# A hybrid decoder layer on one core: five blocks of one 426-column tile in place of three blocks of two 355-column tiles, with the small weight parts kept in HBM

## The chip, the core and the metric

The kernel runs on one core of a Trainium2 chip. The metric is the device time of one execution in microseconds (us); the runs of the kernel before give 3005.64 to 3007.39, median 3006.2. The profile shows one execution by engine: PE (matrix products), PEld (the loads of its weights), DVE (vector), ACT (scalar), POOL, and SP, which here issues all DMA transfers in order.

## What is computed

One layer of a decoder for 2,064 prompt rows (16 meta tokens and 2,048) and 8 × 8 sample rows, 2,128 rows in all, 1,024 channels, float32. Cut to what matters:

```python
h = rmsnorm(x, norm1_g)
z = h @ w_in                                   # 1024 -> 5 x 1024
a = za * sigmoid(zg)                           # GLU
a = layernorm(causal_dwconv(a, width 31) + conv_b)
a = silu(a) @ w_conv_out
p = multiscale_pool(zp)                        # trailing means over 2, 4, 8, 16 rows, less the row
p = einsum(p by 4 groups, w_pool) * pool_scale
m = sigmoid(gate_a) * a + sigmoid(gate_b) * p
x = x + m @ w_out
h2 = rmsnorm(x, norm2_g)
up = causal_dwconv(h2 @ w_up, width 3)         # 1024 -> 2 x 2816
x = x + (gelu(g) * v) @ w_down
y = rmsnorm(x, final_g)
```

The last rows of each causal operation are outputs too.

## The kernel before

Channels lie on the 128 partitions, in chunks; rows of x are the columns of every tile. The columns are cut into three blocks of 708, 708 and 712 (`WIDTHS`), each of two column tiles of 354 or 356, which lie in the two banks of one PSUM tile (4 of these). The sample rows are in block 2 (`SBLK`).

Every float32 operand of a product is held as two float32r parts: a rounded part and the rest, `hi` and `lo` for activations, `wh` and `wl` for weights. `gemm` makes three products per 128 channels of depth, wl·hi, wh·lo and wh·hi. For a weight of 1,024 channels by 128 outputs (512 KB) and one block these are 24 products for each of the two column tiles. Weights are loaded anew in each block: `w_loads` issues the load into `raw`, `w_split` lets ACT copy it to `wh` and DVE subtract it to `wl`, up to four weights ahead (`LEAD`).

The products are in units, one per output chunk: G (gate and value of the convolution branch), PG (pooling input, `w_pool`, merge gates), C (`w_conv_out`), WO (`w_out`), and FF, which is made of up-projections and of groups of the down-projection, DN. `join` lets the first few units of a stage run in turn, chunk by chunk, as their operands come about. Before the first block's norms and around the second norm of blocks 0 and 2 the two column tiles go one after the other (`SPLIT`): the products of one run while the other's norm is made. Block 1's G shares weights with block 0's in `G_first`.

A norm squares the chunks on ACT, adds them on DVE (`sumsq`), and in `rstd_ps` takes sums over partitions by small float32 matmuls with `ones`, ten small DVE operations on a tile `rs`, and small matmuls with the unit matrix in `cst`; `rstd_of` copies the result by ACT. `norm1_rstd` (task r1) and `h_make` (tasks h1 and h1b) make the first norm of a block, `norm2` the second, `conv_norm` and `silu` the convolution branch's, `final` the last one. The normalized x of a block is dropped after G and made again for PG (h1b), from loads of x.

The order of all work is written by the program itself: units in a list, and beside them tasks that are stepped by a forecast of each engine's time (`Pace`, `drip`, `force`). A unit that needs a task forces it to its end before its first product, so the task's small matmuls come ahead of these products in the PE's order. On SP a raw load waits until the split of the weight that had its place is done.

Of the kernel before, what the change touches and what calls it, by code (L numbers as in the profile page):

```python
# [32 lines left out]
NBLK = 3  # L33
SBLK = 2
TOT = NP_ALL + NSAMP
_W = TOT // NBLK // 4 * 4
WIDTHS = [_W + 4 * (i >= NBLK - (TOT - NBLK * _W) // 4) for i in range(NBLK)]
assert sum(WIDTHS) == TOT and all(w % 4 == 0 for w in WIDTHS)
# [10 lines left out]
S_SLOTS = 52  # L49
S_COLS = max(HC + WMAX, WMAX + 2)  # L50
W_BUFS = 4
RAW_BUFS = 2
F_GROUPS = (6, 5, 5, 6)
LEAD = 4
# [3 lines left out]
RESERVE = 3  # L58
# [3 lines left out]
LAST_GROUPS = (8, 7, 7)  # L62
OWN = 4
POOL_ORDER = (1, 0, 3, 2)
BOTH, FIRST, SECOND = (0, 1), (0,), (1,)
SPLIT = (FIRST, SECOND)
# [50 lines left out]

class Task:
# [5 lines left out]
def trunk(ctx: ExitStack, tc: tile.TileContext, A, O):  # L124
# [5 lines left out]
    ppool = ctx.enter_context(tc.tile_pool(name="ppool", bufs=4, space=bass.MemoryType.PSUM))  # L130
# [16 lines left out]
    def room(k):  # L147
        """Waits until k more tiles fit, beside a few for the work that can't wait."""

        def ok():  # L150
            held[:] = [t for t in held if sys.getrefcount(t) > 3]
            return len(held) + k <= S_SLOTS - RESERVE

        if not ok():
            yield "room", ok

    def PSUM():
        return pace.alloc("ps", 4, ppool.tile([P, 2, 512], F32, tag="ps", name=nm("ps")))
# [58 lines left out]
    def hw(b):  # L217
        return WIDTHS[b] // 2

    def cols(b, ts_):  # L220
        return ts_[0] * hw(b), (ts_[-1] + 1) * hw(b)

    def sb(ap, b, ts_):
        """The columns of a tile that belong to the column tiles ts_, in the shape of ps_of."""
        c0, c1 = cols(b, ts_)
        return ap[:, c0:c1].rearrange("p (a c) -> p a c", a=len(ts_))

    def ps_of(ps, b, ts_, off=0):
        return ps[:, : len(ts_), off : off + hw(b)]

    R = {}

# [1 line left out]
    wq = []  # L234
    wsplits = {}
    wstate = {"load": 0, "split": 0, "done": 0}

    def w_loads():
        while wstate["load"] < min(len(wq), wstate["done"] + RAW_BUFS):
            src, n = wq[wstate["load"]][:2]  # L240
            raw = pace.alloc("raw", RAW_BUFS, wpool.tile([P, n], F32, tag="raw", name=nm("raw"), bufs=RAW_BUFS))
            load(raw, src)
            wq[wstate["load"]].append(raw)
            wstate["load"] += 1

    def w_split(i):
        while len(wq[i]) < 3:
            yield "cond", lambda: len(wq[i]) > 2
        n, raw = wq[i][1], wq[i][2]
        wh = pace.alloc("wh", W_BUFS, wpool.tile([P, n], F32R, tag="wh", name=nm("wh")))  # L250
        wl = pace.alloc("wl", W_BUFS, wpool.tile([P, n], F32R, tag="wl", name=nm("wl")))
        wq[i].append((wh, wl))
        yield "at", max(pace.ready(wh), pace.ready(raw))
        act(wh, raw, AF.Copy)
        yield at(wh)
        tt(wl, raw, wh.bitcast(F32), ALU.subtract)
        wstate["done"] += 1
        w_loads()

    def w_start(first):  # L260
        w_loads()
# [5 lines left out]
    def w_ahead(i, first):  # L267
        """Weights up to number i are split when this returns; more are under way, first is the oldest still in use."""
# [10 lines left out]
    def gemm(ps, w, pairs, rng, woff=0):  # L279
# [12 lines left out]
    def rng(b, ts_, halo=0):  # L292
        h = hw(b)
        return [(t * h, (t + 1) * h + halo) for t in ts_]

# [4 lines left out]
    def rsums(acc, n):  # L300
        """Mean over all channels of acc, whose columns [0, n) hold sums over the channel chunks, on every partition."""
        ps = PSUM()
        k = 1 if n <= 512 else 2
        for t in range(k):
            mm(ps[:, t, : n // k], ones, acc[:, t * (n // k) : (t + 1) * (n // k)], True, True, 4.0)
        return ps[:, :k, : n // k]

    def rstd_ps(src, n):
        """1 / sqrt(mean of squares + eps) of each column, on every partition.

        The columns' sums go to a column on their own partition each, there a first guess from the exponent, a step of
        third order and a Newton step follow, and a product with the unit matrix takes the result to all partitions."""
        acc = yield from sumsq(src, n)
        yield at(acc)
        halves = 1 if n <= 512 else 2
        h = n // halves
        cuts = [(t, c) for t in range(halves) for c in [*range(0, h - P + 1, P)] + [h - P] * (h % P > 0)]
        k = len(cuts)
        ps = PSUM()
        for j, (t, c) in enumerate(cuts):  # L320
            mm(ps[:, 0, j : j + 1], acc[:, t * h + c : t * h + c + P], ones[:, :1], True, True, 64.0)
# [4 lines left out]
        ts(v, ps[:, 0, :k], EPS, None, ALU.add)  # L326
# [9 lines left out]
        for j, (t, c) in enumerate(cuts):  # L336
            mm(ps[:, t, c : c + P], w[:, 1, j : j + 1].to_broadcast([P, P]), cst[:, O_ID : O_ID + P], True, True, 4.0)
        yield at(ps)
        return ps[:, :halves, :h]

    def rstd_of(src, n):
# [3 lines left out]
        act(wide(out, ps), ps, AF.Copy)  # L345
# [3 lines left out]
    def wide(x, ps):  # L349
        return x.rearrange("p (a c) -> p a c", a=ps.shape[1])  # L350

    def sumsq(src, n):
        """Squares of the chunks, summed; each chunk is added after the start of the next."""
# [24 lines left out]
    def staggered(first):  # L378
        """The rest after rounding, of chunk after chunk, each one after the start of the next."""
# [15 lines left out]
    def norm1_first(ts_):  # L395
        """First norm of block 0, one column tile at a time."""
        c0, c1 = cols(0, ts_)
        xs = [x_load(0, c, c0, c1) for c in range(KC)]
# [6 lines left out]
        r = yield from rstd_of(src, c1 - c0)  # L405
        if ts_[0] == 0:
            R["h", 0] = [(S(WIDTHS[0], F32R), S(WIDTHS[0], F32R)) for _ in range(KC)]

        def first(c):
            stt(xs[c], xs[c], col(O_N1 + c), r, ALU.mult, ALU.mult)  # L410
            act(R["h", 0][c][0][:, c0:c1], xs[c], AF.Copy)
            return xs[c], *(x[:, c0:c1] for x in R["h", 0][c])
# [43 lines left out]
    def past(b, key, c, rows, src, bufs):  # L456
        """The loader of a chunk's rows before the sample rows, in the block that holds these."""
# [10 lines left out]
    def gate_post(b, c, ts_, ps):  # L468
        if ts_[0] == 0:
            R["t", b, c] = S(WIDTHS[b])  # L470
        act(sb(R["t", b, c], b, ts_), ps_of(ps, b, ts_), AF.Tanh, scale=0.5)
        yield

    def value_post(b, c, ts_, ps):
        n, h, t = NPB[b], hw(b), R["t", b, c]
        if ts_[0] == 0:
            a = S(HC + n)
            pcopy(a[:, :HC], ahist[:, c, :])
            R["a", b, c] = [a, None, 0]
# [800 lines left out]
```

## Time and profile before

| | us |
|---|---|
| median of 3 runs (lowest, highest) | 3006.2 (3005.64, 3007.39) |
| span of the profiled execution | 3004.0 |
| PE busy | 2963.5 |
| DVE busy | 2162.5 |
| ACT busy | 970.3 |
| POOL busy | 87.9 |
| DMA share, moved | 25.4%, 251.6 MB |

The profiled execution's span is 2.2 us less than the median of the runs, which also hold what lies around the span. The PE's records overlap by the depth of its pipeline (a record lasts 326 ns, and one begins every 163), so the time of a product is read from starts or from the count in a stretch. Where PE waited, a row names the engine, tile and line that released it.

```profile
PE   7999999999999999999999999999999999999998
DVE  7999998789899856633698899986763366535356
ACT  4212234343222333522332322333352244313132
DMA  4211221422221223123332122222322242222223
```

Each digit is the busy share, in tenths, of a fortieth of the span.

### The profile page before, as it was taken

What the parts mean: (1) busy time and instruction counts of PE and PEld (TensorE: products, weight loads), DVE (VectorE), ACT (ScalarE), POOL (GpSimd) and SP (SyncE); (2) the same over time, 40 slices, a digit from 0 to 9 for tenths busy, and PEclk for the clock granted to TensorE, in tenths of its full rate; (3) what the DMA queues carried; (4) which work ended last, traced back from release to release, by engine and by line L of the source; (5) the groups of instructions that cost most, each with busy time, mean ns of one, the idle gap of its engine ahead of it and who ended that gap; (6) DMA issues with size and microseconds to landing.
All of it is one profiled execution on the core that took longest, in us unless ns stands there. A gap on an engine that the chain in (4) does not pass through costs nothing.

```text
span 3004.0 us, 43514 instructions
## 1 busy us (share of the span) xinstructions
PE 2963.5 (99%) x18156; PEld 2956.5 (98%) x18156; DVE 2162.5 (72%) x2958; ACT 970.3 (32%) x1311; POOL 87.9 (3%) x185
## 2 busy tenths in 40 slices
PE   7999999999999999999999999999999999999998
PEld 7999999999999999999999999999999999999998
DVE  7999998789899856633698899986763366535356
ACT  4212234343222333522332322333352244313132
POOL 0111000010000000000010000000000000000000
PEclk9999999999999999999999999999999999999999
DMA  4211221422221223123332122222322242222223
GB/s 166 75 36 60 71 70 47 156 80 60 74 71 55 79 86 119 64 78 117 122 99 68 61 80 65 66 74 75 122 86 77 96 137 74 79 68 77 71 77 114
DMA packets 95235, 251.64 MB, mean 84 GB/s; under 512 B 22080, under 2 KB 30400, under 8 KB 95040
## 3 DMA queue, kind: packets, MB, share of 16 engines
q1 hardware_dynamic: 95040, 248.88, 25.4%
q8 instruction: 142, 2.33, 0.3%
q14 instruction: 53, 0.43, 0.0%
HBM read 236.09 MB, written 12.75 MB: 83 GB/s over the span
## 4 chain that ended last, share of the span: by engine, by line
PE 97%; DVE 2%; ACT 1%; issue 0%; DMA 0%; SPq 0%; DVEq 0%; ACTq 0%
PE ps L200 97%; DVE s L171 1%; ACT s L183 1%; DVE s L167 1%; DMA s<-in_x 0%; DVE rs L171 0%; DVE wl L167 0%; ACT wh L183 0%; DVE rs L167 0%; SPq L192 0%; DVE rs L179 0%; DVE uw L167 0%; DVE rs L177 0%; DVEq L1258 0%; ACTq L183 0%
## 5 line engine op out<-in xcount | busy, mean ns | idle before, releaser
L200 PE MATMUL ps<-s,wh 128*128 128x354 f32 (+2 forms) x11904 | 2907.9, 326 | 8.0 <-DVE s L167 7.9
L200 PEld LDWEIGHTS ps<-s,wh 128*128 128x128 f32 x11904 | 2097.9, 189 | 10.7 <-DVE s L167 10.4
L200 PE MATMUL ps<-s,wl 128*128 128x356 f32 (+2 forms) x5952 | 1944.6, 327 | 6.8 <-ACT s L183 3.7
L200 PEld LDWEIGHTS ps<-s,wl 128*128 128x128 f32 x5952 | 1122.8, 189 | 8.9 <-ACT s L183 7.3
L171 DVE SCALAR_TENSOR_TENSOR s<-s,half,s 128x708 f32<-128x708 f32 (+1 forms) x720 | 626.7, 928 | 0.0
L167 DVE TENSOR_TENSOR wl<-raw,wh 128x1024 fp32r<-128x1024 f32 (+4 forms) x416 | 476.6, 1147 | 193.2 <-ACT wh L183 190.3
L183 ACT ACTIVATE wh<-raw 128x1024 fp32r<-128x1024 f32 (+4 forms) x416 | 412.3, 994 | 550.6 <-PE ps L200 410.5
L183 ACT ACTIVATE s<-s 128x708 fp32r<-128x708 f32 (+7 forms) x424 | 296.7, 710 | 548.0 <-DVE s L171 397.1
L167 DVE TENSOR_TENSOR s<-s,s 128x708 f32<-128x708 f32 (+7 forms) x453 | 358.5, 801 | 93.6 <-ACT s L183 89.4
L171 DVE SCALAR_TENSOR_TENSOR s<-ps,cst,s 128x708 f32<-128x708 f32 (+3 forms) x276 | 254.6, 924 | 189.4 <-ACT sf L183 109.7
L183 ACT ACTIVATE s<-ps,cst 128x708 f32<-128x708 f32 (+3 forms) x138 | 113.5, 825 | 457.6 <-PE ps L200 457.6
L167 DVE TENSOR_TENSOR s<-s,ps 128x708 f32<-128x708 f32 (+3 forms) x160 | 123.1, 779 | 144.9 <-PE ps L200 144.1
L183 ACT ACTIVATE s<-ps 128x708 f32<-128x708 f32 (+3 forms) x121 | 82.5, 690 | 396.4 <-PE ps L200 396.3
L171 DVE SCALAR_TENSOR_TENSOR s<-s,s 128x708 f32<-128x708 f32 (+2 forms) x96 | 85.3, 891 | 44.0 <-ACT s L183 42.4
L171 DVE SCALAR_TENSOR_TENSOR s<-s,ps 128x708 f32<-128x708 f32 (+5 forms) x65 | 44.0, 698 | 91.2 <-PE ps L200 90.5
L171 DVE SCALAR_TENSOR_TENSOR s<-s,cst,s 128x708 f32<-128x708 f32 (+3 forms) x112 | 83.5, 767 | 27.9 <-ACT s L183 14.8
L167 DVE TENSOR_TENSOR s<-s 128x722 f32<-128x722 f32 (+7 forms) x60 | 53.2, 886 | 17.0 <-ACT s L183 15.6
L171 DVE SCALAR_TENSOR_TENSOR sc<-sa,cst,sc 128x64 f32<-128x64 f32 x232 | 47.1, 278 | 0.3
L183 ACT ACTIVATE s<-s,half 128x708 f32<-128x708 f32 (+1 forms) x48 | 46.5, 975 | 0.8
L188 POOL COPY s<-phist 128x15 f32<-128x15 f32 x24 | 12.8, 534 | 1014.8 <-ACT s L183 1007.3
L188 POOL CAST s<-hhist 128x2 fp32r<-128x2 f32 x48 | 19.2, 416 | 642.9 <-PE ps L200 555.3
L200 PEld LDWEIGHTS ps<-ones,s 128*128 128x128 f32 x144 | 18.6, 197 | 11.8 <-issue 11.7
(43 smaller groups left out, 273.4 us busy)
## 6 DMA issues: line engine op xcount, KB each, us to landing
raw<-in_w_up SPq DMA_DIRECT2D x132, 512.0 KB, 3.3
raw<-in_w_in SPq DMA_DIRECT2D x112, 512.0 KB, 3.3
raw<-in_w_out SPq DMA_DIRECT2D x40, 512.0 KB, 3.3
s<-in_x SPq DMA_DIRECT2D x40, 354.0 KB, 6.1
raw<-in_w_co SPq DMA_DIRECT2D x24, 512.0 KB, 3.3
raw<-in_w_dn SPq DMA_DIRECT2D x32, 384.0 KB, 3.1
s<-in_x SPq DMA_DIRECT2D x32, 356.0 KB, 5.9
raw<-in_w_dn SPq DMA_DIRECT2D x24, 448.0 KB, 3.4
```

Source lines behind the costliest of these rows:

```text
L167: nc.vector.tensor_tensor(out=out, in0=a, in1=b, op=op)
L171: nc.vector.scalar_tensor_tensor(out=out, in0=a, scalar=s, in1=b, op0=op0, op1=op1)
L183: nc.scalar.activation(out, a, func, **kw)
L188: nc.gpsimd.tensor_copy(out, a)
L200: nc.tensor.matmul(out, lhsT=lhsT, rhs=rhs, start=start, stop=stop)
```

## The change

There are five blocks of 424, 426, 426, 426 and 426 columns, one column tile each, so that a unit has 24 products of one width. PSUM has eight tiles of one bank; there are 5 places for `wh` and `wl` (before 4), 3 for `raw` (2), 76 for activations (52). The halves (`SPLIT`, `G_first`) are gone: every norm covers its whole block.

A weight's `wl` is computed when the weight is used first (136 subtracts in place of 416) and stored to a tile `keep_` in HBM (136 stores); the other 544 uses load it back straight into `wl`. `wh` is copied by ACT from `raw` at each of the 680 uses (416 before).

The order of the stages is new: G(0), PG(0), G(1), PG(1), C(0), WO(0), FF(0), C(1), WO(1), G(2), FF(1), PG(2), C(2), WO(2), G(3), FF(2), PG(3), C(3), WO(3), G(4), FF(3) without its last DN group, PG(4), C(4), WO(4), that group, FF(4). silu of blocks 0 and 1 may begin eight units ahead of C (two before, in block 0). The task h1b, which begins at `mark["up_end", b]`, begins in block 4 right at PG(4), since no DN group stands there any more.

```diff
-NBLK = 3
-SBLK = 2
+NBLK = 5
+SBLK = NBLK - 1
+WIDTHS = [424, 426, 426, 426, 426]
-S_SLOTS = 52
+S_SLOTS = 76
-W_BUFS = 4
-RAW_BUFS = 2
+W_BUFS = 5
+RAW_BUFS = 3
+PS_BUFS = 8
-LEAD = 4
+LEAD = W_BUFS
-RESERVE = 3
+RESERVE = 4
...
+            q.lo = pace.alloc("wl", W_BUFS, wpool.tile([P, n], F32R, tag="wl", name=nm("wl")))
+            q.known = q.key in kept
+            if q.known:
+                load(q.lo.bitcast(F32), kept[q.key])
...
+        act(q.hi, q.raw, AF.Copy)
+        if not q.known:
+            yield at(q.hi)
+            tt(q.lo, q.raw, q.hi.bitcast(F32), ALU.subtract)
+            if q.again:
+                stores.append(q)
...
+        if len(stores) > 1 or (stores and q.known):
+            p = stores.pop(0)
+            kept[p.key] = dpool.tile([P, p.n], F32, tag=f"keep_{len(kept)}", name=f"keep_{len(kept)}")
+            store(kept[p.key], p.lo.bitcast(F32))
...
-            for i, (c0, c1) in enumerate(rng):
-                o = ps[:, i, : c1 - c0]
-                mm(o, wl[:, w0 : w0 + P], xh[:, c0:c1], k == 0, False)
-                mm(o, wh[:, w0 : w0 + P], xl[:, c0:c1], False, False)
-                mm(o, wh[:, w0 : w0 + P], xh[:, c0:c1], False, k == last)
+            o = ps[:, : c1 - c0]
+            mm(o, wl[:, w0 : w0 + P], xh[:, c0:c1], k == 0, False)
+            mm(o, wh[:, w0 : w0 + P], xl[:, c0:c1], False, False)
+            mm(o, wh[:, w0 : w0 + P], xh[:, c0:c1], False, k == last)
...
+    G(0, H1(0), False)
+    PG(0, H1(0), False)
+    mark["G", 1] = len(units)
+    G(1, H1(1), False)
+    PG(1, H1(1), False)
+    for b in range(NBLK):
+        if b > 1:
+            PG(b, H1B(b), True)
+        C(b)
+        WO(b)
+        if b == NBLK - 1:
+            DN(b - 1, *late)
+        elif b:
+            mark["G", b + 1] = len(units)
+            G(b + 1, H1(b + 1), True)
+        else:
+            mark["G", 2] = len(units)
+        late = FF(b, b == NBLK - 2)
...
-        add_task(("s", b), silu(b), mark["mid", b] if b else mark["C", 0] - 2, [("cv", b)])
+        add_task(("s", b), silu(b), mark["mid", b] if b > 1 else mark["C", b] - 8, [("cv", b)])
```

What this makes of the order is seen on PE where WO(1) passes into G(2). Before, `ps_12457` is the first norm of block 2, made inside WO(1), and `ps_12861` the second norm of block 1, made inside G(2); `ps_12464` and `ps_12542` are products of WO(1), `ps_12777` and `ps_12793` of G(2):

```order
L200 MATMUL ps_12394<-s_12168,wh_12158 128x354
L200 MATMUL ps_12457<-ones,s_12307 128x1 x6
L200 MATMUL ps_12464<-s_11393,wl_12239 128x354
...
L200 MATMUL ps_12464<-s_12168,wh_12158 128x354
L200 MATMUL ps_12457<-cst,rs_12517 128x128 x6
L200 MATMUL ps_12542<-s_11393,wl_12299 128x354
...
L200 MATMUL ps_12793<-s_12686,wh_12664 128x356
L200 MATMUL ps_12861<-ones,s_12302 128x1 x6
L200 MATMUL ps_12777<-s_12746,wl_12514 128x356
...
L200 MATMUL ps_12793<-s_12746,wh_12664 128x356
L200 MATMUL ps_12861<-cst,rs_12886 128x128 x6
L200 MATMUL ps_12777<-s_12754,wl_12514 128x356
```

The same place in the change, where `ps_8295` is the last unit of WO(1), `ps_8337` the first norm of block 2, `ps_8374` the second norm of block 1, and `ps_8444` the first unit of G(2):

```order
L204 MATMUL ps_8295<-s_7997,wh_8124 128x426
L204 MATMUL ps_8295<-s_8005,wl_8122 128x426
L204 MATMUL ps_8295<-s_8006,wh_8124 128x426
L204 MATMUL ps_8295<-s_8005,wh_8124 128x426
L204 MATMUL ps_8337<-ones,s_8160 128x1 x4
L204 MATMUL ps_8337<-cst,rs_8345 128x128 x4
L204 MATMUL ps_8374<-ones,s_8093 128x1 x4
L204 MATMUL ps_8374<-cst,rs_8385 128x128 x4
L204 MATMUL ps_8444<-s_8380,wl_8156 128x426
```

Between `ones` and `cst` stood 48 products in the one norm and 18 in the other; now both norms stand after the last product of WO(1), with no product inside them. It is the same from WO(2) to G(3) and from WO(3) to G(4).

On PE from WO(0) to FF(0), before, `ps_5147` is the second norm of one column tile of block 0 and `ps_5154` a unit of WO(0) for the other:

```order
L200 MATMUL ps_5115<-s_4820,wh_4997 128x354
L200 MATMUL ps_5147<-ones,s_4903 128x1 x3
L200 MATMUL ps_5154<-s_4488,wl_5066 128x354
...
L200 MATMUL ps_5154<-s_4820,wh_5065 128x354
L200 MATMUL ps_5147<-cst,rs_5183 128x128 x3
L200 MATMUL ps_5203<-s_4488,wl_5068 128x354
```

and in the change `ps_4638` is the last unit of WO(0), `ps_4684` the norm of the block, `ps_4786` the first unit of FF(0):

```order
L204 MATMUL ps_4638<-s_4354,wl_4477 128x424
L204 MATMUL ps_4638<-s_4355,wh_4478 128x424
L204 MATMUL ps_4638<-s_4354,wh_4478 128x424
L204 MATMUL ps_4684<-ones,s_4448 128x1 x4
L204 MATMUL ps_4684<-cst,rs_4689 128x128 x4
L204 MATMUL ps_4786<-s_4708,wl_4513 128x426
```

A unit of 24 products between the norm's two halves is gone. From DN(0) to C(1) the small matmuls of block 0's last norm stand as close together.

On SP, in the middle of a stage, before, with what each transfer waits for (DMAHW is the lane that it uses, DVE the split of the weight that had the place):

```order
L192 DMA raw_2557<-in_w_in 128x1024 [waits DMAHW5_49,DVE_49]
L192 DMA raw_2632<-in_w_in 128x1024 [waits DMAHW6_49,DVE_49]
L192 DMA raw_2705<-in_w_in 128x1024 [waits DMAHW7_49,DVE_49]
L192 DMA raw_2754<-in_w_pool 128x512 [waits DMAHW0_49,DVE_49]
L192 DMA raw_2817<-in_w_in 128x1024 [waits DMAHW1_49,DVE_49]
```

and in the change, with `keep_` the stored parts in HBM:

```order
L196 DMA raw_12628<-in_w_in 128x1024 [waits DMAHW5_49,Activation_49]
L196 DMA wl_12630<-keep_1778 128x1024 [waits DMAHW4_49,PE_49]
L196 DMA raw_12670<-in_w_in 128x1024 [waits DMAHW7_49,Activation_49]
L196 DMA wl_12672<-keep_1845 128x1024 [waits DMAHW6_49,PE_49]
L196 DMA raw_12720<-in_w_in 128x1024 [waits DMAHW1_49,Activation_49]
L196 DMA wl_12722<-keep_1848 128x1024 [waits DMAHW0_49,PE_49]
```

Each weight has two transfers in place of one; the second waits for the PE to be done with the weight that had the place in `wl`.

More of the change, by code (lines that the diff above doesn't have):

```diff
@@ L31 @@
 MAGIC = float(0x5F3759DF)
-NBLK = 3
-SBLK = 2
+NBLK = 5
+SBLK = NBLK - 1
 TOT = NP_ALL + NSAMP
-_W = TOT // NBLK // 4 * 4
-WIDTHS = [_W + 4 * (i >= NBLK - (TOT - NBLK * _W) // 4) for i in range(NBLK)]
-assert sum(WIDTHS) == TOT and all(w % 4 == 0 for w in WIDTHS)
+WIDTHS = [424, 426, 426, 426, 426]
+assert sum(WIDTHS) == TOT and all(w % 2 == 0 for w in WIDTHS)
 COL0 = [sum(WIDTHS[:i]) for i in range(NBLK)]
@@ L115, in __init__ @@
         self.joined = False
+class Weight:
+    def __init__(self, key, src):
+        self.key, self.src, self.n = key, src, src.shape[1]
+        self.raw = self.hi = self.lo = None
+        self.known = self.again = False
 class Task:
@@ L215, in hcol @@
         return half[:, o - O_LG : o - O_LG + 1]
[L217 to L229, printed above, removed]
     R = {}
     wq = []
+    kept = {}
     wsplits = {}
-    wstate = {"load": 0, "split": 0, "done": 0}
+    wstate = {"load": 0, "split": 0, "done": 0, "first": 0}
@@ L238, in w_loads @@
     def w_loads():
[L239 to L243, printed above, removed]
+        while True:
+            i = wstate["load"]
+            if i >= min(len(wq), wstate["done"] + RAW_BUFS, wstate["first"] + LEAD):
+                break
+            q = wq[i]
+            n = q.n
+            q.raw = pace.alloc("raw", RAW_BUFS, wpool.tile([P, n], F32, tag="raw", name=nm("raw"), bufs=RAW_BUFS))
+            load(q.raw, q.src)
+            q.lo = pace.alloc("wl", W_BUFS, wpool.tile([P, n], F32R, tag="wl", name=nm("wl")))
+            q.known = q.key in kept
+            if q.known:
+                load(q.lo.bitcast(F32), kept[q.key])
@@ L244, in w_loads @@
             wstate["load"] += 1
     def w_split(i):
[L247 to L256, printed above, removed]
+        q = wq[i]
@@ L260, in w_start @@
+    stores = []
     def w_start(first):
+        wstate["first"] = first
         w_loads()
@@ L300, in rsums @@
     def rsums(acc, n):
[L302 to L306, printed above, removed]
+        ps = PSUM()[:, :n]
+        mm(ps, ones, acc[:, :n], True, True, 4.0)
+        return ps
     def rstd_ps(src, n):
@@ L393, in staggered, with norm1_first @@
             yield
[L395 to L398 removed]
+    def norm1_first():
+        xs = [x_load(0, c) for c in range(KC)]
         yield at(xs[0])
@@ L916, in PG, with G @@
-    def PG(b, nd, ga):
+            W(("in", part * KC + c), A["w_in"][part * KC + c]), lambda: R["h", b], b, lambda ps: post(b, c, ps), nd,
+            pre=pre, drop=("h", b) if drop else None,
+        )
+    def G(b, nd, drop):
+        i = len(units)
+        for c in range(KC):
+            in_unit(b, 1, c, gate_post, nd)
+            in_unit(b, 0, c, value_post, nd, past(b, "sa", c, HC, "st_conv", 3), drop and c == KC - 1)
+        for u in units[i + 1 : i + JOIN]:
+            u.joined = True
@@ L917, in zp, with PG @@
+    def PG(b, nd, joined):
         def zp(c):
@@ L926, in mmf @@
                     box.append(ps)
-                    yield from gemm(ps, w, [R["p", b, 2 * g + k] for k in range(2)], rng(b, BOTH), d * 2 * P)
+                    yield from gemm(ps, w, [R["p", b, 2 * g + k] for k in range(2)], 0, WIDTHS[b], d * 2 * P)
                 for k in range(2):
@@ L940, in PG @@
             zp(zs[k])
-        if b:
+        if joined:
             join(i)
@@ L967, in C, with WO @@
                 drop=("s", b) if c == KC - 1 else None,
             )
-            if not ga and c == 2:
+            if c == 2:
                 join(mark["C", b])
-    def WO(b, parts):
+    def WO(b):
         mark["WO", b] = len(units)
-        for ts_ in parts:
-            for c in range(KC):
-                std_unit(
-                    W(A["w_out"][c]), lambda: R["m", b], b, ts_,
-                    lambda ps, c=c, ts_=ts_: add_post(b, c, ts_, ps, "x1n"), (("x", b),), wait=c == 0,
-                    drop=("m", b) if ts_ == parts[-1] and c == KC - 1 else None,
-                )
@@ L982, in up @@
-    def up(b, m, w, nd, ts_=BOTH):
+        for c in range(KC):
+            std_unit(
+                W(("out", c), A["w_out"][c]), lambda: R["m", b], b, lambda ps, c=c: add_post(b, c, ps, "x1n"),
+                (("x", b),), wait=c == 0, drop=("m", b) if c == KC - 1 else None,
+            )
+    def up(b, m):
         f = m % FC
         std_unit(
-            w, lambda: R["h2", b], b, ts_, lambda ps: (g_post if m >= FC else v_post)(b, f, ts_, ps), nd, halo=2,
-            pre=past(b, "sf", m, 2, "st_ffn", 3) if ts_[-1] == 1 else None,
-            drop=("h2", b) if m == 2 * FC - 1 and ts_[-1] == 1 else None,
-        )
@@ L1010, in FF, with after @@
-    def FF(b, parts, last_parts):
-        mark["FF", b] = len(units)
-        ws = [w_up(0), w_up(FC), w_up(1)]
-        for ts_ in parts:
-            i = len(units)
-            for m, w in zip((0, FC, 1), ws):
-                up(b, m, w, (("h2", b, ts_),), ts_)
-            join(i)
-        nd = (("h2", b, parts[-1]),)
+        for c in range(KC):
+            def after(ps, c=c):
+                yield from add_post(b, c, ps, "x2n" if f1 == FC else None)
+                if c == KC - 1:
+                    for f in range(f0, f1):
+                        del R["f", b, f]
+            std_unit(
+                W(("dn", c, f0), A["w_dn"][c][:, f0 * P : f1 * P]), lambda: [R["f", b, f] for f in range(f0, f1)],
+                b, after, (), c == 0,
+            )
+            if f1 == FC and c + 1 == JOIN:
+                join(first)
@@ L1100, in under_way @@
             del wsplits[j]
-        quiet = any(mark["WO", b] <= now["i"] < mark["FF", b] + 2 for b in parts)
+        quiet = any(mark["WO", b] <= now["i"] < mark["FF", b] + 2 for b in (0, NBLK - 1))
         ws = [wsplits[j] for j in sorted(wsplits)]
@@ L1155, in trunk @@
             nc.gpsimd.memset(hhist[i].bitcast(F32), 0.0)
+        last = {q.key: i for i, q in enumerate(wq)}
+        for i, q in enumerate(wq):
+            q.again = last[q.key] > i
         oldest = [u.w for u in units]
@@ L1173, in trunk @@
                 force(name)
-            turns = [u.mm(wq[u.w][3]) for u in group]
+            turns = [u.mm((wq[u.w].hi, wq[u.w].lo)) for u in group]
             while turns:
```

350 lines of the change are left out of this document (125 added, 225 removed).

## The prediction

> **What bounds the kernel now.** I read the page's busy times first, then its chain of waits, then what the PE waited for, and last the stretches in which nothing disturbs the PE.
>
> ```profile
> PE 2963.5 (99%) x18156; PEld 2956.5 (98%) x18156; DVE 2162.5 (72%) x2958; ACT 970.3 (32%) x1311; POOL 87.9 (3%) x185
> PE ps L200 97%; DVE s L171 1%; ACT s L183 1%; DVE s L167 1%; DMA s<-in_x 0%; DVE rs L171 0%; DVE wl L167 0%; ACT wh L183 0%; DVE rs L167 0%; SPq L192 0%; DVE rs L179 0%; DVE uw L167 0%; DVE rs L177 0%; DVEq L1258 0%; ACTq L183 0%
> PE ps L200 <- DVE s L167: 19.3, 7, 9.6
> PE ps L200 <- DVE rs L171: 7.1, 5, 2.0
> PE ps L200 <- ACT s L183: 3.7, 3, 1.8
> PE ps L200 <- DVE s L171: 3.0, 4, 1.1
> ```
>
> The PE is busy for 2963.5 of 3004.0 us and carries 97% of the chain. Its waits (total, times, longest) come to 33 us, 9.6 of them in one wait. So two things can change the time: what one product costs, and new waits of the PE. Work taken from DVE or ACT is worth nothing by itself.
>
> What a product costs is read where the PE runs without a gap: the first two windows hold only 354-column products at a granted clock of 0.50 and of 1.00, the third only 358-column ones (columns: length, PE busy and records, clock, DMA share, GB/s). Under them stand starts of products at the half clock.
>
> ```profile
> 37.20:41.00 3.80, 3.80 (x14) 0.50 0.03 10
> 100.00:300.00 200.00, 200.00 (x1232) 1.00 0.13 44
> 2490.00:2600.00 110.00, 110.00 (x670) 1.00 0.28 84
> 37.49 0.50 PE L200 MATMUL ps<-s,wl 128*128 128x354 f32 x1
> ...
> 38.38 0.50 PE L200 MATMUL ps<-s,wl 128*128 128x354 f32 x1
> ...
> 39.26 0.50 PE L200 MATMUL ps<-s,wl 128*128 128x354 f32 x1
> ```
>
> Less the records cut at a window's edges (about two each), a product takes 200/1230 = 162.6 ns at 354 columns and 110/668 = 164.7 at 358. Over all 17,856 products (mean 355.4 columns) I take 163.2. At the half clock six starts span 1.77 us, 295 ns each. If the clock alone counted, 354 columns would take half of that, 147.5. So at full clock some 15 ns of each product are not columns.
>
> **The change part by part.** *Fewer, wider products.* The work in columns is the same (6.346 against 6.343 million); the 17,856 products become 14,880 of 426.3 columns. The trace has no product wider than 358. One bound is that the 15 ns are paid per product: 426.3 × 147.5/354 = 177.6, plus 15.1, is 192.7 ns, and 14,880 × 192.7 − 17,856 × 163.2 = 2867 − 2914 = −47 us. The other is that they grow with the columns: 163.2 × 426.3/355.4 = 195.8 ns, and −1 us. The two windows give 0.5 ns a column with an error of 0.1, where per product means 0.42 and growth 0.46: they don't decide. I take −46, since a cost that vanishes when the clock halves looks like a step between two instructions that needs a fixed real time rather than like slower columns, and keep 0 for the range.
>
> The Trainium skill ("TensorE: Matmul & The Clock Gate", section "Back-to-back issue gap") gives an isolated gap of N/2.4 + 2.5 ns on a warm clock, 150.4 ns here; the trace disagrees, with 163. By that rule only 2.5 ns are fixed and the gain is 2,976 × 2.5 = 7 us.
>
> *Weight parts.* DVE's subtract runs 136 times in place of 416; 544 weights come back from HBM instead, and ACT copies 680 high parts in place of 416.
>
> ```profile
> L167 DVE TENSOR_TENSOR wl<-raw,wh 128x1024 fp32r<-128x1024 f32 x316 | 385.7, 1222 | 168.1 <-ACT wh L183 165.7
> L183 ACT ACTIVATE wh<-raw 128x1024 fp32r<-128x1024 f32 x316 | 332.5, 1054 | 407.2 <-PE ps L200 305.3 <-issue 76.1 <-DMA raw<-in_w_in 11.7
> raw<-in_w_in SPq DMA_DIRECT2D x112, 512.0 KB, 3.3
> 0.00:20.00 20.00, 6.49 (x22) 5.77 (x23) 12.35 (x30) 11.41 (x21) 1.09 (x10) 1.00 0.80 266
> 645.00:2150.00 1505.00, 1505.00 (x9258) 1504.12 (x9258) 1156.07 (x1562) 474.53 (x584) 30.43 (x68) 1.00 0.25 82
> ```
>
> DVE loses 280 × 1.15 us (all 416 averaged 1147 ns) = 322 us, but its other work comes in five pieces for three, with a fixed share in each: I put its total near 2050 of 3000. ACT gains 264 copies of about 1 us and ends near 45%. Both lie under the PE; credit zero. The cover is the PE's 4.63 us a weight (24 products × 192.7 ns), in which ACT has one copy to make and DVE, in blocks 0 and 1, a subtract for part of the weights.
>
> SP now issues 1,662 transfers in place of 662, in order. A 512 KB raw load and a 512 KB read-back each 4.63 us are 1.05 MB, 226 GB/s; the first 20 us moved 266 at a share of 0.80, so the share would be about 0.68, against 0.25 now. A read-back waits for the PE's weight five back, a raw load for ACT's copy three back; with 3.3 us to land they are issued some 4 weights, 18 us, ahead. Queued behind a read-back that waits are the other loads of x; that matters only where x is wanted at once (below). I credit and charge nothing, and keep −0 to +200 us (a rival) for it.
>
> *Waits that go.* The rows below are the first norm's second half, silu before C(0), and block 2's second norm.
>
> ```profile
> 33.48 0.94 PE L200 MATMUL ps<-cst,rs 128*128 128x128 f32 x6 [2.04 <-DVE rs L171]
> 36.17 0.66 PE L200 MATMUL ps<-s,wl 128*128 128x354 f32 x1 [1.76 <-ACT s L183]
> 41.33 0.62 PE L200 MATMUL ps<-s,wh 128*128 128x354 f32 x2
> 492.37 0.96 PE L200 MATMUL ps<-s,wh 128*128 128x354 f32 x2 [4.59 <-DVE s L167]
> 2479.68 0.40 PE L200 MATMUL ps<-s,wl 128*128 128x358 f32 x1 [1.14 <-DVE s L171]
> 2480.80 0.40 PE L200 MATMUL ps<-s,wl 128*128 128x358 f32 x1 [0.39 <-DVE s L171]
> 2484.47 0.59 PE L200 MATMUL ps<-s,wh 128*128 128x358 f32 x2 [1.31 <-DVE s L167]
> ```
>
> Block 0 is one tile: the 3.8 us before 36.17 go, with the half clock up to 41.5 (half of 5.3), but 70 more columns of eight chunks are loaded and squared before the first product, which I put 2 us later: −4.5. silu(0) now has block 1's projections between itself and C(0), and starts eight weights ahead instead of two: 4.6 plus some 1.5 of half clock, of which I count −5. Block 2's 3.3 us go (in the last block, group DN(3) stands between norm and FF(4)): −3.3.
>
> *Waits that come.* In before a norm's small matmuls had products of another tile or unit between them; in the changed order there are four places where they stand back to back. What such a chain takes is on show once, at the end of before:
>
> ```profile
> 2989.92 0.49 PE L200 MATMUL ps<-s,wh 128*128 128x356 f32 x2
> 2990.45 0.53 DVE L167 TENSOR_TENSOR s<-s,ps 128x356 f32<-128x356 f32 x1 [0.95 <-PE ps L200]
> 2991.06 0.50 ACT L183 ACTIVATE s<-s 128x356 f32<-128x356 f32 x1 [2.98 <-DVE s L167]
> 2991.59 0.53 DVE L167 TENSOR_TENSOR s<-s,s 128x356 f32<-128x356 f32 x1 [0.18 <-ACT s L183]
> 2992.27 0.80 PE L200 MATMUL ps<-ones,s 128*128 128x1 f32 x6 [1.86 <-DVE s L167]
> 2993.11 0.16 DVE L177 TENSOR_SCALAR rs<-ps 128x3 f32<-128x3 f32 x1 [0.98 <-PE ps L200]
> ...
> 2995.11 1.65 PE L200 MATMUL ps<-cst,rs 128*128 128x128 f32 x6 [2.04 <-DVE rs L171]
> 2996.80 0.58 DVE L171 SCALAR_TENSOR_TENSOR s<-s,cst,ps 128x356 f32<-128x356 f32 x1 [1.75 <-PE ps L200]
> ```
>
> From the last product (2990.4) to the first scaled chunk it is 6.4 us.
>
> - WO(0) to FF(0): the 6.4, then ACT's copy (0.5), the scaling (0.58), the high part (0.5), that is 8 us, and some 2 of half clock, less 1 for the small matmuls that I count below: 9. In before the two halves of this norm cost the place as much as block 2's, 3.3: +5.7.
> - DN(0) to C(1): the final norm's small matmuls stand before C(1), and silu(1) is only ending then: a chain of about the same length and half clock: +9, with 4 as the low end if silu's first chunks are ready.
> - WO(b) to G(b+1), b = 1, 2, 3: two norms' chains, of the next block's first norm and of this block's second, follow the last product. They overlap up to the first's rows in `rs` (2 us each on DVE, 2993.11 to 2995.1): about 8 us without the small matmuls but with 2 of half clock, three times: +24. Low end 4 each, if the first norm's sums are done before the PE gets there; high end 12, if the loads of x behind a waiting read-back are late.
> - PG(4): the normalized x of block 4 is remade at the moment when it is wanted, because DN(3) has moved behind WO(4). The load of x, then one chunk's scaling and splitting:
>
> ```profile
> s<-in_x SPq DMA_DIRECT2D x40, 354.0 KB, 6.1
> L171 DVE SCALAR_TENSOR_TENSOR s<-s,cst,s 128x354 f32<-128x354 f32 x32 | 18.2, 581 | 3.1 <-ACT s L183 3.1
> ```
>
> Four chunks of 213 KB land in some 4 us, and 2 us of DVE and ACT follow: +6.
> - The first pooling weight in blocks 2 to 4 comes one unit after the joined group: +1 each, +3, a guess between 0 and 6.
>
> *Small things.* 32 more records of float32 matmuls at about 0.11 us (six of them take 0.94 us in the row at 33.48, each beginning before the one ahead ends): +3.6. The tail is 426 instead of 356 columns: +1.
>
> *Sum:* −46 − 4.5 − 5 − 3.3 + 5.7 + 9 + 24 + 6 + 3 + 3.6 + 1 = −6.5 us. The profiled execution spans 3004.0 us, 2.2 under the median 3006.2 of the runs (3005.64 to 3007.39), so its own scale and theirs differ by a constant: 2997.5 in the span, **2999.7 us** in the runs. About 45 us are won in the stream of products, and four fifths are given back where one block hands over to the next.
>
> **The rivals.** First, *the 15 ns grow with the columns* (195.8 ns): the products win nothing, the waits stay, 2999.7 + 45 = about 3044, slower. The 0.5 ns a column of the two windows speaks for it, the clean 295 ns at the half clock against. It decides from an interval of 193.1 ns on, where the gain falls under 40 us. It is nearly what the Trainium skill's issue-gap rule, named above, would do to this case: 2.5 ns fixed, the rest per column.
>
> Second, *the waits are shorter*: r1's sums come before WO ends and silu(1) is ready, so that half of the 45 us of the first four bullets stays covered: about 2977. For it: DVE has a third of its time free. Against it: the order puts nothing between the small matmuls.
>
> Third, *the weights come too late*. Two loads a weight fall behind the PE if the queue sustains under 226 GB/s; at 210 each of the 620 weights (14,880/24) takes 5.0 us in place of 4.63, +220 us, 3220. Against it: 266 GB/s at 0.80 busy in the first 20 us.
>
> Fourth, *more waits at block transitions* than I found in the order: eight places by 3 us, 3024.
>
> Fifth, *the interval hardly depends on the columns*, since weight loads fill 98% of the span too: then 426 columns take their 177.6 ns plus little, say 180, and the time is near 2810. The 2.1 ns between the two windows speak against it. That page of the Trainium skill also states sustained figures of 81 ns at 128 columns and 131 at 512, which would be flatter still; the 163 ns at 354 contradict them.
>
> **How the numbers follow.** The forecast has 0.47, with its own range of ±12 us (2988 to 3012) from the ends given for the new waits. Growth with columns has 0.15, shorter waits 0.19, more waits 0.08, weights late 0.06, flat interval 0.05. Runs can be told apart by about 0.2%, 6 us: 3000.2 to 3012.2 counts as no change. The forecast sits at that border and gives half of its chance to faster, a third to the same, a sixth to slower; with 0.24 from the second and fifth rivals and 0.29 from the others that makes faster 0.47, the same 0.16, slower 0.37. The range leaves out the flat interval below and late weights above, with a few points of their neighbours: 2958 to 3050.
>
> **What would show it.** Right: a window of pure 426-column products at 192 to 193.5 ns; PE idle of 6 to 10 us at the three WO to G transitions and at WO(0) to FF(0), each followed by some 4 us at clock 0.50, with DVE named as releaser; a DMA share of 0.65 to 0.7; no wait for read-backs in midstream. Wrong: an interval of 195 or more, or of 185 or less; PE waiting for DMA `wl` or ACT `wh`; or transitions with 2 us of idle.

## The result, and the profile after

The changed kernel takes 3029.05 us (median of 4 runs, 3028.0 to 3030.94) against 3006.55: ratio 1.0077, 95% interval 1.0063 to 1.0091. It is slower by 22.5 us, where 2999.7 was forecast; the range 2958 to 3050 held the time. From the page after (busy times, then the main DMA queue), and what PE waited for:

```profile
PE 2961.8 (98%) x15210; PEld 2864.5 (95%) x15210; DVE 1993.6 (66%) x3755; ACT 1281.0 (42%) x1959; POOL 118.2 (4%) x313
q1 hardware_dynamic: 239040, 696.74, 65.2%
PE ps L204 <- DVE s L171: 23.9, 9, 10.7
PE ps L204 <- DVE rs L175: 21.2, 14, 2.1
PE ps L204 <- ACT s L187: 11.4, 4, 5.7
PE ps L204 <- ACT wh L187: 0.5, 1, 0.5
```

DVE lost 169 us of work (some 110 were foreseen) and DMA moves 2.8 times as much, at a share near the 0.68 forecast; neither is the bound. PE is as busy as before with 3,000 products fewer, and waits for 57 us in place of 33. Windows of undisturbed PE (the first of 424 columns, the second mostly of 428), and one behind a wait:

```profile
100.00:200.00 100.00, 100.00 (x521) 1.00 0.66 227
1020.00:1120.00 100.00, 100.00 (x516) 1.00 0.61 218
912.00:915.50 3.50, 3.50 (x14) 0.50 0.04 18
```

Less two cut records, a product takes 192.7 and 194.6 ns. From the starts of all products at full clock it is 192.8 at 424 columns, 194.6 at 426 and 194.4 at 428, against 163.0, 163.3 and 164.7 at 354, 356 and 358. So the stream of products costs 2891 us and cost 2917. WO(1) to G(2) is the place with both norms behind the last product:

```profile
903.17 0.95 PE L204 MATMUL ps<-ones,s 128*128 128x1 f32 x8
906.16 2.08 PE L204 MATMUL ps<-cst,rs 128*128 128x128 f32 x8 [2.04 <-DVE rs L175]
908.02 1.71 PE L204 MATMUL ps<-ones,s 128*128 128x1 f32 x8
911.77 2.08 PE L204 MATMUL ps<-cst,rs 128*128 128x128 f32 x8 [2.04 <-DVE rs L175]
913.50 0.70 PE L204 MATMUL ps<-s,wl 128*128 128x426 f32 x1
```

Two chains of 2.04 us on DVE stand one after the other, with PE idle. The granted clock falls to 0.50 within the first and stays there for 10 us:

```profile
905.80:916.00 10.20, 7.80 (x31) 0.50 0.63 217
```

So the 8 us lost here are 4.1 of idle PE and 4.0 of half clock. The other places of the changed kernel, from the timeline (WO(0) to FF(0), DN(0) to C(1), where the view ends at the sixth record of the second row, and PG(4)):

```profile
494.70 1.05 PE L204 MATMUL ps<-ones,s 128*128 128x1 f32 x8 [3.67 <-DVE s L171]
497.79 2.08 PE L204 MATMUL ps<-cst,rs 128*128 128x128 f32 x8 [2.04 <-DVE rs L175]
501.85 0.69 PE L204 MATMUL ps<-s,wl 128*128 128x426 f32 x1 [1.99 <-ACT s L187]
...
820.80 1.87 PE L204 MATMUL ps<-ones,s 128*128 128x1 f32 x8 [5.16 <-DVE s L171]
824.71 1.65 PE L204 MATMUL ps<-cst,rs 128*128 128x128 f32 x6 [2.04 <-DVE rs L175]
...
2469.14 0.72 PE L204 MATMUL ps<-s,wl 128*128 128x426 f32 x1 [5.72 <-ACT s L187]
```

Time lost by PE beside an even spacing of products, half clock included, worked out from the starts in both traces:

| place | before | after | change | forecast |
|---|---|---|---|---|
| stream of products | 2917 | 2891 | −26 | −46 |
| start and first norm, with the first product | 14.9 | 10.7 | −4.1 | −4.5 |
| silu(0) before C(0) | 6.3 | 0 | −6.3 | −5 |
| block 2's second norm | 4.3 | 0 | −4.3 | −3.3 |
| WO(0) to FF(0) | 4.3 | 11.5 | +7.2 | +5.7 |
| DN(0) to C(1) | 0 | 13.1 | +13.1 | +9 |
| WO to G, three times | 0 | 23.4 | +23.4 | +24 |
| PG(4) | 0 | 11.3 | +11.3 | +6 |

Small matmuls, pooling weights, tail and losses too small to list make up the rest, about 8.

### The profile page after: what moved, and what is told of

Its sections match the earlier page's. It is cut to its first block, busy times and chain, and to the rows that moved or that the text cites. A ratio compares the mean times of both kernels' runs of the same rounds, so it can differ in the third digit from the quotient of the medians.

```text
span 3026.8 us, 41309 instructions
## 1 busy us (share of the span) xinstructions
PE 2961.8 (98%) x15210; PEld 2864.5 (95%) x15210; DVE 1993.6 (66%) x3755; ACT 1281.0 (42%) x1959; POOL 118.2 (4%) x313
## 4 chain that ended last, share of the span: by engine, by line
PE 96%; DVE 3%; DMA 1%; ACT 1%; issue 0%; SPq 0%; DVEq 0%; ACTq 0%
PE ps L204 96%; DVE s L175 1%; DVE s L171 1%; ACT s L187 0%; DVE rs L175 0%; DMA out_ffn_s<-sf 0%; DVE rs L171 0%; DVE rs L183 0%; DVE wl L171 0%; DMA s<-in_x 0%; DMA sf<-in_st_ffn 0%; SPq L196 0%; DVE rs L181 0%; ACT wh L187 0%; DVE uw L171 0%
## 5 line engine op out<-in xcount | busy, mean ns | idle before, releaser
L204 PE MATMUL ps<-s,wh 128*128 128x426 f32 (+2 forms) x9920 | 2741.4, 357 | 1.3 <-DVE s L171 0.8
L204 PEld LDWEIGHTS ps<-s,wh 128*128 128x128 f32 x9920 | 1877.6, 189 | 62.0 <-DVE s L171 2.4
L204 PE MATMUL ps<-s,wl 128*128 128x426 f32 (+2 forms) x4960 | 1778.7, 359 | 11.4 <-ACT s L187 11.4
L204 PEld LDWEIGHTS ps<-s,wl 128*128 128x128 f32 x4960 | 939.4, 189 | 43.5 <-ACT s L187 10.9
L187 ACT ACTIVATE wh<-raw 128x1024 fp32r<-128x1024 f32 (+3 forms) x680 | 660.1, 977 | 410.1 <-DMA raw<-in_w_up 172.7
L175 DVE SCALAR_TENSOR_TENSOR s<-s,half,s 128x426 f32<-128x426 f32 (+2 forms) x1200 | 697.4, 642 | 2.3 <-ACT s L187 2.0
L187 ACT ACTIVATE s<-s 128x426 f32<-128x426 f32 (+3 forms) x604 | 332.6, 558 | 577.9 <-DVE s L175 365.0
L171 DVE TENSOR_TENSOR s<-s,s 128x426 fp32r<-128x426 f32 (+3 forms) x659 | 387.4, 599 | 169.4 <-ACT s L187 163.1
L175 DVE SCALAR_TENSOR_TENSOR s<-ps,cst,s 128x426 f32<-128x426 f32 (+2 forms) x440 | 284.3, 647 | 196.1 <-ACT s L187 110.9
L171 DVE TENSOR_TENSOR wl<-raw,wh 128x1024 fp32r<-128x1024 f32 (+3 forms) x136 | 152.0, 1126 | 24.3 <-ACT wh L187 18.5
```

Source lines behind the costliest of these rows:

```text
L171: nc.vector.tensor_tensor(out=out, in0=a, in1=b, op=op)
L175: nc.vector.scalar_tensor_tensor(out=out, in0=a, scalar=s, in1=b, op0=op0, op1=op1)
L187: nc.scalar.activation(out, a, func, **kw)
L204: nc.tensor.matmul(out, lhsT=lhsT, rhs=rhs, start=start, stop=stop)
```

## The experiments

**The price of a product.** Two kernels leave out the layer and run streams of 24-product units with operands split beforehand. The first changes width and what runs beside.

```diff
+# columns, first column, loads beside, vector operations and scalar operations a unit beside, units
+PLAN = [
...
+    (424, 0, 0, 0, 0, 24), (426, 0, 0, 0, 0, 24), (428, 0, 0, 0, 0, 24), (430, 0, 0, 0, 0, 24),
...
+    (356, 0, 1, 0, 0, 24), (426, 0, 1, 0, 0, 24), (428, 0, 1, 0, 0, 24),
+    (356, 0, 0, 5, 0, 24), (426, 0, 0, 5, 0, 24), (426, 0, 0, 0, 5, 24),
```

> The layer is left out: only units of 24 products, as a weight of the layer makes them, 24 units to a stretch, with the operands already split; first with nothing beside them at 354, 356, 358, 424, 426, 428, 430, 256, 320, 480 and 512 columns, then 356, 426 and 428 with the kernel's two 512 KB loads a unit, then with five vector or five scalar operations a unit, then with all. After the change a product takes 194.4 ns against the 192.7 forecast. Theory A, the read-backs: transfers into the same memory slow the products. Then the quiet stretch at 426 gives 192.5 to 193 and the one with loads 194.5. Theory B, steps of four columns: 354, 358, 426 and 430 cost as much as 356, 360, 428 and 432 (0.8 ns too much), and what is left over the columns, 14.7 ns at 355, grows a little with the width, to 16 at 426. Then 426 and 428 take the same 194.4 with or without loads, and 424 takes 192.7. Theory C, vector and scalar traffic: the quiet stretches give 193, those with vector or scalar operations 194.5.

Windows at 426 columns: nothing beside, then the loads, then the vector operations, then the scalar ones:

```profile
510.00:610.00 100.00, 100.00 (x514) 1.00 0.00 1
1350.00:1450.00 100.00, 100.00 (x513) 1.00 0.64 226
1670.00:1770.00 100.00, 100.00 (x513) 1.00 0.00 1
1780.00:1885.00 105.00, 105.00 (x538) 1.00 0.00 1
```

That is 195.3 to 195.9 ns in all four: 226 GB/s of loads change nothing, nor do DVE or ACT. Theories A and C fall. Theory B's steps of four fall as well: by starts 424, 426, 428 and 430 columns took 193.3, 195.5, 192.3 and 195.6, no steps of 0.8, and 512 took 232.2, which no excess of 16 gives (213 + 16 = 229). The stretches with everything beside starved on their vector operations and say nothing on the products.

The second kernel changes widths and the layout of the operands.

```diff
+# columns, columns from tile to tile, first column, order of tiles
+PLAN = [
...
+    (354, 742, 0, 2),
...
+    (426, 456, 0, 1),
...
+    (426, 464, 8, 1),
...
+    (128, 520, 0, 1),
...
+    (512, 520, 0, 1),
```

> The layer is left out: streams of units of 24 products with nothing beside them, 10 units to a stretch, at many widths and with operands laid out as in the kernels (tiles 742 or 456 columns apart, in a mixed order) and at distances of 464, 480, 512 and 520 columns. Theory D, slower columns: averaged over layouts a product takes 5.6 ns plus 0.443 ns a column, so 162.4 at 354, 194.2 at 426, 118.9 at 256, 232.3 at 512 and 62 at 128, and the layout moves single widths by up to 2 ns either way. Theory E, as forecast, a fixed 15 ns: 121.8 at 256 and 228.4 at 512, and 192.6 at 426 in the mean of the layouts. If layout alone made the miss, the tiles 456 columns apart give 194.4 at 426 and another distance gives 192.7 or less in all orders.

Windows at 354, 426 (tiles 456 apart), 426 (464 apart), 128, 256 and 512 columns:

```profile
62.00:98.00 36.00, 36.00 (x224) 1.00 0.00 1
555.00:597.00 42.00, 42.00 (x219) 1.00 0.00 1
1020.00:1064.00 44.00, 44.00 (x228) 1.00 0.00 1
1720.00:1744.00 24.00, 24.00 (x218) 1.00 0.01 1
1774.00:1799.00 25.00, 25.00 (x214) 1.00 0.01 1
1930.00:1981.00 51.00, 51.00 (x221) 1.00 0.00 0
```

With two records off, 162.2, 193.5, 194.7, 111.1, 117.9 and 232.9 ns. From 256 columns up that is a line of about 0.445 ns a column and 4.5 ns a product: Theory D, and not the fixed 15 ns of Theory E (121.8 and 228.4). A straight fit through all stretches of both kernels that run without a gap gives 0.441 and 6.2, so the fixed part is known to a nanosecond or two. At 128 columns Theory D misses too: 111 ns is a floor, the same at 192 columns by starts. Layout moves 426 columns between 193.3 and 195.6, to no 192.7.

**The read-backs.** Left out, with the stores that they read, first:

```diff
-            if q.known:
-                load(q.lo.bitcast(F32), kept[q.key])
...
+        if q.known:
+            q.lo = q.hi
```

> The changed kernel without read-backs and stores of small parts: from a weight's second use on, the large part is multiplied three times in place of the small one, so the small parts' share of the sums is left out. Everything else stands. Theory A (read-backs slow the products): the product falls from 194.4 to about 193 ns, and the time by 15 to 25 us, to 3005 to 3015. Theory B (width and steps of four): the products stay at 194.2 to 194.6 ns and the time within 5 us of 3029, the small rest from waits at the three places where loads of x are queued.

3005.0 us (3003.54 to 3005.75), ratio to the kernel before 0.9994 (0.9984 to 1.0004). The time fell as Theory A has it, and the products did not: 192.9, 194.8 and 194.4 ns. The 24 us are the three WO to G waits, which are gone: the planner, which counts the transfers, now places the next block's norm inside WO. In WO, 16 loads of x come on top of the weights. The 13 us in which they begin, in the changed kernel and then in this one (the clock, DMA share and GB/s come last):

```profile
866.00:879.00 13.00, 13.00 (x68) 12.60 (x67) 2.99 (x5) 4.03 (x6) 0.37 (x2) 1.00 0.97 350
```

```profile
853.00:866.00 13.00, 13.00 (x68) 12.60 (x67) 4.82 (x8) 3.43 (x6) 0.00 (x0) 1.00 1.00 350
```

The transfer engines are as full without the read-backs as with them, but the loads come 12 us earlier. Is x late on the chip when there are read-backs, or only in the planner's reckoning? Next the planner is kept from counting read-backs:

```diff
-                load(q.lo.bitcast(F32), kept[q.key])
+                nc.sync.dma_start(out=q.lo.bitcast(F32), in_=kept[q.key])
```

> The changed kernel with all its read-backs, but the planner no longer counts them (the forecast of the transfer engine is not advanced by a read-back). The three WO to G then have products between the norms' small matmuls again, as in the kernel without read-backs, which took 3005.0. If read-backs cost nothing on the chip and only shift the order that the planner writes, this takes 3005 to 3008 and the three waits are gone. If the traffic itself makes x late, the waits stay, and the time is above 3020.

3047.7 us, ratio 1.0137 (1.012 to 1.0154): the order has products between the small matmuls, and PE now waits inside WO. SP's queue, ACT and PE there:

```profile
866.93 4.07 SPq L196 DMA_DIRECT2D s<-in_x  x8
...
872.40 0.33 SPq L242 DMA_DIRECT2D wl<-keep  x1
872.93 3.23 SPq L196 DMA_DIRECT2D s<-in_x  x6
```

```profile
879.01 2.37 ACT L187 ACTIVATE s<-s 128x426 f32<-128x426 f32 x4 [9.27 <-DMA s<-in_x]
```

```profile
887.09 1.87 PE L204 MATMUL ps<-ones,s 128*128 128x1 f32 x8 [6.20 <-DVE s L171]
```

So x is really late, and the planner was right to move the norm. Late by its place in SP's queue, or by the traffic? The same kernel with the loads of x issued by ACT:

```diff
-        load(x, A["x"][c, :, COL0[b] + c0 : COL0[b] + c1])
+        (nc.scalar if b else nc.sync).dma_start(out=x, in_=A["x"][c, :, COL0[b] + c0 : COL0[b] + c1])
+        pace.put("dma", size(x) * P * 4 / 340.0, [x], [], late=2000.0)
```

> The kernel whose planner does not count the read-backs (3047.7 us), in the same order, with one edit more: from block 1 on the loads of x are issued by ACT in place of SP. Theory F, the queue: x came late there because its loads stood on SP behind read-backs that wait for the PE. Then the waits of about 10, 9 and 8 us with half clock inside WO(1) to WO(3), and the rest of 3 to 5 us behind them, go, and the time falls to 3005 to 3015. Theory G, the traffic: x is late since the transfer engines are 65% busy. Then the loads take as long from ACT, the waits stay at 6 us each, and the time is above 3035.

3058.0 us, ratio 1.0167 (1.0152 to 1.0182). ACT's queue, ACT and PE:

```profile
871.17 1.73 ACTq L371 DMA_DIRECT2D s<-in_x  x3
878.24 0.56 ACT L187 ACTIVATE s<-s 128x426 f32<-128x426 f32 x1 [6.15 <-DMA s<-in_x]
```

```profile
890.02 1.87 PE L204 MATMUL ps<-ones,s 128*128 128x1 f32 x8 [11.24 <-DVE s L171]
```

The time is above the 3035 of Theory G, but the run doesn't decide between the two, since the loads leave no earlier. ACT comes to them in the order of its own work at 866.07, behind an operation that had waited 3.2 us for DVE, and SP had come to them at 866.93. The kernel without read-backs tells more. There SP has the same loads at the same place of its list, behind the 193rd load into `raw`, and PE has got as far (its 4,000th product starts at 802.7 us, with read-backs at 802.3):

```profile
853.58 3.77 SPq L196 DMA_DIRECT2D s<-in_x  x8
```

They leave 13 us earlier. The 16 loads then take 3.7 to 6.6 us to land, 5.2 in the median; with read-backs on SP it is 3.6 to 6.2, and 5.7. What holds SP back is in its waits that end from 855 to 867 us, with read-backs (total, times, longest; L242 issues the read-backs):

```profile
SPq L242 <- PE ps L204: 11.4, 3, 3.8
```

So x is late because it leaves late, behind read-backs that wait for PE: Theory F, by the traces, though no run takes the loads out of every queue that waits. That the wait grew from 6 to 11 us neither theory had; ACT, which makes the squares, now also issues the loads, and the last five of the 16 (878.25 to 884.46) stand between squares that wait for earlier ones. On the faster order below the same edit costs 11.5 us:

> The kernel with the four edits to the order (2986.5 us), with the loads of x from block 1 on issued by ACT in place of SP. Its PE waits for x nowhere by more than 2 us, so if Theory F holds there is little left to win: 2983 to 2988. ACT spends about 0.4 us to issue each of some 120 loads, which is hidden unless ACT is late for a norm; then up to 2995.

2998.0 us (ratio 0.9973, 0.9961 to 0.9984): above even the 2995 allowed, so in this order the loads of x are better left to SP.

**The waits.** The next block's first norm begun one stage earlier, so that its loads are spread over C and WO:

```diff
-            add_task(("r1", b + 1), norm1_rstd(b + 1), mark["WO", b] if b else 2)
+            add_task(("r1", b + 1), norm1_rstd(b + 1), mark["C", b] if b else 2)
```

> The changed kernel with the first norm of blocks 2 to 4 begun with C of the block before in place of WO. It keeps all else. If the three waits from WO to G (8.0, 8.3 and 7.0 us with the half clock) come from the two norms standing behind the last product of WO, they go, and the time falls by 18 to 23 us, to about 3008. If the loads of x or the vector engine are what is late there, the waits stay within 3 us of what they were, and the time within 8 us of 3029.

3009.7 us (3007.51 to 3011.81), ratio 1.0011 (1.0002 to 1.002): 19 us of the 23 are gone, read-backs and all. WO(1) is as full as it was (first line), and at WO(1) to G(2) the one norm left there waits for 0.19 us, so the traffic by itself does not make PE wait:

```profile
866.00:903.00 37.00, 37.00 (x193) 35.98 (x192) 17.35 (x31) 16.23 (x24) 1.08 (x4) 1.00 0.88 322
```

```profile
908.45 0.95 PE L204 MATMUL ps<-ones,s 128*128 128x1 f32 x8
911.44 1.16 PE L204 MATMUL ps<-cst,rs 128*128 128x128 f32 x8 [0.19 <-DVE rs L175]
```

Then the planner's idea of a product:

```diff
-        pace.put("pe", size(out) * rate / 2.4 + 2.5, [out], [lhsT, rhs])
+        pace.put("pe", size(out) * rate / 2.4 + 16.5, [out], [lhsT, rhs])
```

> The changed kernel with the planner's cost of a product raised by 14 ns, nothing else. Background work of the vector engine is then written earlier among the products. If silu(1) is late at C(1) because the planner gives the vector engine too little in the time of a product, the 13 us at DN(0) to C(1) fall to 2 or 3, and the time to about 3018, with the three WO to G waits shorter by up to 4 us each, since the first of the two norms gets products inside it in blocks 3 and 4. If not, it stays within 4 us of 3029.

3021.7 us, ratio 1.005 (1.0035 to 1.0065), where 3018 was expected. The 13 us before C(1) are gone (first line; the norm has products inside it), against a new wait of 5 us with its half clock near 270 (second line), where the convolution norm's mean is now written too early:

```profile
831.31 1.16 PE L204 MATMUL ps<-cst,rs 128*128 128x128 f32 x8 [0.18 <-DVE rs L175]
```

```profile
271.79 1.19 PE L204 MATMUL ps<-s,ones 128*128 128x424 f32 x2 [2.87 <-DVE s L171]
```

All four places at once; beside the two edits above:

```diff
-        for c in range(2, KC):
+        for c in range(2, KC - GA.get(b, 0)):
...
+    GA = {1: 4}
...
+        for c in range(KC - GA.get(b + 1, 0), KC):
+            in_unit(b + 1, 3, c, ga_post, H1(b + 1), drop=c == KC - 1)
         late = FF(b, b == NBLK - 2)
...
-                add_task(("h1b", b + 1), h_make(b + 1, True), mark["up_end", b], [("r1", b + 1)])
+                add_task(("h1b", b + 1), h_make(b + 1, True), mark["up_end", b] - 8 * (b == NBLK - 2), [("r1", b + 1)])
```

> The changed kernel with four edits: the first norms of blocks 2 to 4 begun with C; the planner's cost of a product 14 ns higher (N/2.4 + 16.5), near what the chip takes; the remaking of block 4's normalized x begun eight units earlier; four merge-gate units of block 1 moved between WO(0) and FF(0). If the waits account for the loss beside the products, all of the 11.5, 13.1, 23.4 and 11.3 us at WO(0) to FF(0), DN(0) to C(1), the three WO to G and PG(4) go but for some 10: 2980, faster than before by 0.9%. If instead the waits move to other places because the vector engine is late anyway, it stays above 3005.

2986.5 us (2985.22 to 2989.34), ratio 0.9936 (0.9921 to 0.9951). By starts PE's losses fall by 47 us. It is 6 us above the 2980 expected, and 5 of them are the wait near 270. One number more, 12.5 in place of 16.5:

> The kernel with the four edits to the order (2986.5 us), with the planner's cost of a product at N/2.4 + 12.5 in place of 16.5. At 16.5 one wait of 5 us stood near 270 us, where the mean of the first convolution norm is put ahead of the vector engine's work. The lower cost puts that mean 48 products later; the other places keep products between the norms' small matmuls. If that wait comes from the planner's cost it goes: 2980 to 2983. If not, it stays at 2986 within 3 us.

2979.9 us (2978.97 to 2980.36), ratio to the kernel before **0.9913 (0.9899 to 0.9926)**, the fastest here. Its PE and waits:

```profile
PE 2943.8 (99%) x15210; PEld 2846.7 (96%) x15210; DVE 1984.5 (67%) x3755; ACT 1278.9 (43%) x1959; POOL 114.4 (4%) x313
PE ps L204 <- DVE s L171: 12.9, 5, 10.5
PE ps L204 <- DVE rs L175: 6.0, 12, 2.0
PE ps L204 <- ACT s L187: 3.6, 2, 2.5
PE ps L204 <- ACT wh L187: 2.7, 2, 2.4
```

The wait near 270 is gone. With 25 us of waits, 8 fewer than before the change, it is 26 us faster: the gain of the product stream, which the changed order had more than given back, is kept, and the 8 us go to small terms, the added small matmuls among them.

## Why the prediction was wrong

*The products: the step that failed.* The term of −46 us measured −26, two thirds of the 29 us by which the time was missed. I saw 295 ns at the half clock, halved the columns' share to 147.5, and called the other 15 ns fixed. The streams show that halving is not allowed: at full clock a column costs 0.445 ns (0.441 by the straight fit) and not half of 0.833 (0.417). So of the 15 ns some 9 or 10 grow with the columns and 4.5 to 6 are paid per product, which on 2,976 products is 13 to 18 us. The rest of the 26 no run explains. It is no more than layout can move: over layouts 354 and 356 columns took 162.2 to 165.4 ns, and 0.5 ns a product of the kernel before is 9 us. The 0.5 ns a column of the two windows, noted and then set aside as undecided, pointed the right way. The first rival, whose threshold of 193.1 ns was passed, came true by half: the product of 194.3 ns (2891 us over 14,880) lies midway between 192.7 and 195.8, and a gain of nothing would have made 3044. By the isolated spacing that the Trainium skill gives ("TensorE: Matmul & The Clock Gate", section "Back-to-back issue gap"), an estimate for 426 columns is 180 ns. This trace shows 194.6.

*The new waits: right in kind, 10 us too small in all, and made up otherwise.* The places and their cause, small matmuls back to back, are as forecast, and an earlier norm cures WO to G. But that 24 were forecast there and 23.4 came is luck. The forecast had some 6 us of idle PE and 2 of half clock at each. WO(1) to G(2) has 4.1 of idle, its low end, since the norm's sums were done before PE got there, and 4.0 of half clock. The half clock is the mis-sized term: it lasts 10.24 us at five of the six places and 6.83 at one, not some 4, and costs 22 us at all six (by the starts, less the idle time), where the bullets hold about 10. DN(0) to C(1) took 13.1 and not 9: 8.8 of idle in three waits (1.6, 5.2 and 2.0), in the longest of which squares of the final norm stood on ACT behind four operations of silu, and 4.0 of half clock. PG(4) took 11.3 and not 6: the 6.0 of idle were right, 3.4 of half clock had been put at nothing, and 1.9 came at a second wait. WO(0) to FF(0) was 1.5 over, with 7.7 and 3.6.

*The waits that go:* all three went, within 2 us of their sizes.

*The read-backs: a zero that was right in midstream and wrong at WO.* The share, forecast 0.68, is 0.65, and no weight comes late but for one wait of 0.5 us. At WO, leaving the read-backs out wins 24 us. The prediction had named the way, loads of x on SP behind a read-back that waits, and gave it only a high end; by the traces they leave 13 us later for it and take about as long to land. In the changed kernel this acts through the planner, which counts the transfers and so puts the norm behind WO. The prediction took that order from the program and did not name its cause.

*Slower* had 0.37 of my chances, 0.15 of it for the growth of the products' cost, which was half of the truth.

## What to carry to other kernels

Price an instruction at a size that the profile does not hold by a line through sizes measured at the same clock; a difference between two clocks is not a per-instruction cost. When blocks become smaller, list for each hand-over what used to run between a norm's reduction and its use: here these places cost more than the wider products gave, and four edits to the order and the planner's costs gave it back. Count the half clock behind a wait by its length in the trace; it cost as much as the wait at WO to G. Where a load is late, compare when it leaves and how long it takes: here it stood in an in-order queue behind transfers that waited, and the busy share of the DMA engines did not tell.

## What the runs showed of the hardware

- A product of float32r parts: about 0.445 ns a column and 4.5 ns from 256 to 512 columns (0.441 and 6.2 by a straight fit), with a floor near 111 ns (128 and 192 columns); at clock 0.50 it is 0.833 ns a column (295 ns at 354).
- Its time did not change by 0.5 ns under 226 GB/s of loads, or under five vector or scalar operations a unit (195.3 to 195.9 ns at 426 columns).
- It does change by where the operands lie: 426 columns took 193.3 to 195.6 ns over layouts.
- At six hand-overs of the changed kernel, with 4 to 9 us of idle PE each, the clock was at 0.50 for 10.24 us, at one of them for 6.83. Inside the spans of all runs such stretches last 3.41, 6.83, 10.24 or 13.65 us.
- With the transfer engines full (0.92 to 1.00 busy, 318 to 350 GB/s), loads of x of 213 KB landed 3.6 to 6.6 us after issue, with read-backs beside them or without.
